# A hybrid decoder layer: two PSUM pools for the whole program, another pairing of the output tiles, and a later second norm

## The chip, the cores and the metric

The kernel runs on one core of one Trainium2 chip. The metric is the device time of one execution in microseconds (us). The kernel before took 1080.27 us, the median of three runs (1080.08, 1080.27, 1080.79). Its profile was taken in one further execution.

## The reference

One layer on x of 1024 tokens x 1024 channels, in fp32:

```python
u = rms_norm(x, norm1_g)
z = u @ w_in                                  # split into a convolution part and a retention part
y = concat(group_norm(conv(z)), group_norm(retention(z)) * silu(gate))
x = x + y @ w_out
h = relu(rms_norm(x, norm2_g) @ w_up)         # w_up is 1024 x 4096
x = x + (h * h) @ w_down                      # w_down is 4096 x 1024
out = rms_norm(x, final_norm_g)
```

The change touches the line with `w_out` (the tiles of x that it finishes), the second norm, and the two products of the MLP.

## The kernel before, in words

**Number format.** All matmuls of the large products take operands that are split into a high and a low part of fp32r. One product of 512 x 512 by 512 x 512 in one call of `mm` (L395 to L403) into one PSUM bank is 12 matmuls of 128 x 512: four slices of the contracted dimension, times high by high, low by high, high by low. The activations' parts are tiles `U` (`V` for the down product, `y` for the out-projection), the weights' parts `wh` and `wl`. A weight piece `r` comes by DMA; ScalarE (ACT) casts it to `wh`, VectorE (DVE) subtracts to get `wl` (`split_piece`, L168). Sums and differences of weight pieces, `r<-r,r`, are GpSimd's (POOL, `Left.split`). Every call to ACT, DVE and POOL goes through a wrapper, so its line in the profile is L74.

**Layout.** x is kept transposed: `x2[i]` holds 128 channels times 1024 tokens, i = 0 to 7, with two token halves `hs[0]` and `hs[1]`.

**The out-projection** is `group(j)` for j = 0 to 3 (L1059), of 8 steps each. Group j finishes the tiles `x2[j]` and `x2[4 + j]`, first over one half of the contraction and then over the other. `out_evac` (L994) adds a bank to x2 on DVE, squares it on ACT, and adds the square to `sums_[half]` on POOL (`t<-t,t`). The dictionary `todo`, by step number 8j + s, then holds the work that prepares the first MLP product. That one is a Strassen-like scheme: x, scaled by the norm's weights but not yet by its factor, is seen as 2 x 2 blocks (token half by tiles 0 to 3 and 4 to 7), and the seven products, in the order 1, 2, 6, 5, 3, 7, 4 (`MLP_ORDER`), take the operands "11", "21", "t2", "t1", "22", "t3", "t4". Each needs four slices, slice j from tiles j and 4 + j. For j = 3 this preparation runs into the MLP's first products: the list `rest` (L1234) gives what is issued behind each of them. The sums `un` go by DVE's `sum1` to `sum4` (L980 on), a high half of U by ACT's `put_hi`, a low half by DVE's `put_lo`.

**The first MLP pass** (L1249 to L1266) computes the up product for two blocks of 256 hidden channels, in 14 products with a bank each, from pools of the two pairs. Here the second norm's factor is found on the way: `token_roots` (L313) sums the 128 partitions of `sums_` by tiny matmuls with a column of ones and takes roots on ACT, `rnorms` takes reciprocals on DVE, `spread` (L339) brings the factors into two PSUM banks, `r_half`, by matmuls with the identity. `Pair.put` multiplies the finished hidden blocks with them; the two banks stay in use until the last block.

**Down products** (L1268, matmuls at L1276) have an inner dimension of 256 each and a Winograd-like scheme, in which x2 itself collects the products in another basis. `new_basis(i)` (L1003) brings tiles i - 1 and i into it: two POOL subtractions of 128 x 512. Tiles that the MLP needs only later are stored to DRAM meanwhile, `put_aside` (a DMA `k<-x`, L1030), to free SBUF, and read again by `fetch_back` (`x<-k`, L1035). Both are on the SP queue, which works in order, as do the weight loads. After this pass, up and down products alternate, and the last block (L1385) multiplies the remaining hidden channels.

**PSUM** has eight banks of 128 x 512 fp32. Until the out-projection's end they are the pools `pm` and `pr` of four each; then both are closed and `pu` (2), `pd` (4) and `pn` (2, for the factors and later the last block) are opened under the names pm, pr and pn. Instructions of each engine run in the order of issue; semaphores between engines are set by the framework from the tiles that are read and written, and a new pool's tiles wait for those of the closed one.

## Time and profile before

| | |
|---|---|
| runs | 1080.27 us median, 1080.08 to 1080.79 |
| profiled execution, device time | 1081.81 us |
| its span, first to last instruction | 1079.0 us |
| matmuls on TensorE (PE) | 4860, mean granted clock 0.997 |
| instructions on DVE, ACT, POOL | 1246, 904, 366 |
| out-projection's last matmul starts | 442.84 us |
| first MLP pass | 443.70 us to about 486.4 us |
| last block's first matmul starts | 1022.00 us |

The busy share of an engine is an average over stages. A line of a timeline has the start in us from the span's start, the length, the engine, line and operation, out<-in by the program's names, the tile's shape and how many instructions are taken together; a bracket gives idle time of that engine just before, and what ended it. Matmuls overlap their neighbours: their starts, not their lengths, give the pace.

### The profile page before, as it was taken

What the parts mean: (1) busy time and instruction counts of PE and PEld (TensorE: products, weight loads), DVE (VectorE), ACT (ScalarE), POOL (GpSimd) and SP (SyncE); (2) the same over time, 40 slices, a digit from 0 to 9 for tenths busy, and PEclk for the clock granted to TensorE, in tenths of its full rate; (3) what the DMA queues carried; (4) which work ended last, traced back from release to release, by engine and by line L of the source; (5) the groups of instructions that cost most, each with busy time, mean ns of one, the idle gap of its engine ahead of it and who ended that gap; (6) DMA issues with size and microseconds to landing.
All of it is one profiled execution on the core that took longest, in us unless ns stands there. A gap on an engine that the chain in (4) does not pass through costs nothing.

```text
span 1079.0 us, 13854 instructions
## 1 busy us (share of the span) xinstructions
PE 1060.5 (98%) x4860; PEld 881.6 (82%) x4860; DVE 878.7 (81%) x1246; ACT 460.2 (43%) x904; POOL 538.0 (50%) x366
## 2 busy tenths in 40 slices
PE   9999999999989999999999999999999999999997
PEld 7888888887768888788788888888888888888886
DVE  7446546799998656699999989989899899899955
ACT  8211445663435544444433443433343344334453
POOL 6234223255753223559538358267276185384552
PEclk9999999999999999999999999999999999999999
DMA  7111122222223635050121211201301301200204
GB/s 274 62 59 39 40 70 78 75 79 73 78 59 118 215 104 188 1 195 21 48 88 39 69 49 49 79 30 57 90 21 50 98 20 50 88 20 20 69 30 156
DMA packets 39685, 82.25 MB, mean 76 GB/s; under 512 B 4544, under 2 KB 5696, under 8 KB 39616
## 3 DMA queue, kind: packets, MB, share of 16 engines
q1 hardware_dynamic: 39328, 80.85, 23.0%
q8 instruction: 38, 0.62, 0.2%
q10 hardware_dynamic: 288, 0.52, 0.1%
q14 instruction: 31, 0.25, 0.1%
HBM read 71.92 MB, written 9.44 MB: 75 GB/s over the span
## 4 chain that ended last, share of the span: by engine, by line
PE 79%; DVE 10%; POOL 4%; issue 3%; ACT 2%; DMA 1%; DVEq 0%; SPq 0%; POOLq 0%; ACTq 0%
PE b L403 46%; PE b L1276 22%; PE b L357 4%; PE b L1385 4%; DVE wl L74 2%; DVE z L74 2%; POOL z L74 1%; POOL r L74 1%; DVE t L74 1%; DVE x L74 1%; DVE U L74 1%; DVE q L74 1%; DVE xs L74 1%; ACT h L74 1%; DVE m L74 1%
## 5 line engine op out<-in xcount | busy, mean ns | idle before, releaser
L403 PE MATMUL b<-U,wh 128*128 128x512 f32 x1024 | 315.8, 390 | 1.8 <-DVE x L74 1.1
L74 ACT CAST wh<-r 128x512 fp32r<-128x512 f32 x286 | 175.9, 620 | 321.2 <-PE b L403 134.5
L74 DVE TENSOR_TENSOR wl<-r,wh 128x512 fp32r<-128x512 f32 x251 | 231.8, 926 | 91.4 <-ACT wh L74 90.5
L74 POOL TENSOR_TENSOR r<-r,r 128x512 f32<-128x512 f32 x136 | 209.9, 1546 | 116.3 <-DVE wl L74 65.6
L1276 PE MATMUL b<-V,wh 128*128 128x512 f32 x784 | 242.0, 389 | 0.5 <-POOL V L74 0.4
L403 PEld LDWEIGHTS b<-U,wh 128*128 128x128 f32 x1024 | 191.8, 188 | 42.6 <-issue 1.9
L74 DVE TENSOR_TENSOR x<-x,b 128x512 f32<-128x512 f32 (+1 forms) x312 | 195.6, 673 | 30.2 <-PE b L1385 14.2
L403 PE MATMUL b<-U,wl 128*128 128x512 f32 x512 | 199.5, 390 | 0.3 <-POOL wl L74 0.3
L1276 PEld LDWEIGHTS b<-V,wh 128*128 128x128 f32 x784 | 147.1, 188 | 32.3 <-POOL V L74 0.8
L74 POOL TENSOR_TENSOR t<-t,t 128x512 f32<-128x512 f32 x70 | 106.4, 1524 | 97.9 <-ACT t L74 51.9
L1276 PE MATMUL b<-V,wl 128*128 128x512 f32 x392 | 152.5, 389 | 0.0
L74 POOL TENSOR_TENSOR wl<-r,wh 128x512 fp32r<-128x512 f32 x35 | 48.6, 1394 | 160.7 <-ACT wh L74 153.5
L403 PEld LDWEIGHTS b<-U,wl 128*128 128x128 f32 x512 | 96.2, 188 | 21.2 <-POOL wl L74 0.7
L403 PE MATMUL b<-uh,wh 128*128 128x512 f32 x304 | 103.4, 399 | 2.3 <-DVE z L74 2.3
L403 PE MATMUL b<-uh,wl 128*128 128x512 f32 x304 | 100.8, 391 | 1.1 <-DVE wl L74 1.1
L403 PE MATMUL b<-ul,wh 128*128 128x512 f32 x304 | 101.0, 392 | 0.0
L1276 PEld LDWEIGHTS b<-V,wl 128*128 128x128 f32 x392 | 73.5, 188 | 15.2
L74 POOL TENSOR_TENSOR V<-t,V 128x512 fp32r<-128x512 f32 x35 | 49.6, 1416 | 67.3 <-ACT V L74 67.3
L74 DVE TENSOR_TENSOR t<-t,b 128x512 f32<-128x512 f32 x112 | 75.8, 677 | 1.7 <-POOL t L74 1.2
L74 ACT ACTIVATE t<-t 128x512 f32<-128x512 f32 x64 | 40.2, 631 | 79.8 <-DVE t L74 79.2
L74 DVE TENSOR_TENSOR V<-t,V 128x512 fp32r<-128x512 f32 x63 | 70.3, 1116 | 0.0
L403 PEld LDWEIGHTS b<-uh,wl 128*128 128x128 f32 x304 | 57.3, 189 | 13.9 <-DVE wl L74 1.5
(178 smaller groups left out, 1422.1 us busy)
## 6 DMA issues: line engine op xcount, KB each, us to landing
r<-w_up_t SPq DMA_DIRECT2D x64, 256.0 KB, 2.6
r<-w_down_t SPq DMA_DIRECT2D x56, 256.0 KB, 2.7
r<-w_in_t SPq DMA_DIRECT2D x48, 256.0 KB, 2.7
xt<-xT SPq DMA_DIRECT2D x16, 256.0 KB, 5.4
xs<-xT SPq DMA_DIRECT2D x8, 512.0 KB, 4.9
r<-w_out_t SPq DMA_DIRECT2D x16, 256.0 KB, 2.7
x<-xT SPq DMA_DIRECT2D x8, 512.0 KB, 8.9
k<-x SPq DMA_DIRECT2D x6, 512.0 KB, 3.2
```

The lines of the kernel that those rows point to most:

```text
L74: return f(out, *args, **kw)
L357: nc.tensor.matmul(vb[i], a[k][:, i * P : (i + 1) * P], b[k // 2][:, vs], start=(k == 0 and a is uh and b is vh), stop=(k == KT - 1 and a ...
L403: nc.tensor.matmul(b, a[:, k, :], rhs(n, k)[r], start=(start and i == 0), stop=(stop and i == len(ops) - 1),)
L1276: nc.tensor.matmul(b, a, r, start=(i == 0), stop=(i == len(ops) - 1))
L1385: nc.tensor.matmul(z, a, b, start=(k == 0 and t == 0), stop=(k == 3 and t == 2))
```

## The change

Three things are changed together; the instructions of each engine are the same in number.

1. `pm` and `pr` of four banks are kept for the whole program. The factors `r_half`, the first two banks of the last block and the two banks `ends` come from `pm`; `r_half` is cleared ahead of the last block.
2. `new_basis(j)` pairs the tiles j and 4 + j, which one group finishes, and not i - 1 and i. It is called in step 8j + 14 for j < 3, followed by the put-asides of both tiles in step 8j + 15; only `new_basis(3)` is left for the MLP pass, behind product 7 (products are counted from 0). Before, `new_basis(1)` stood in step 16, the put-asides of tiles 0 and 1 in step 17, of 2 in step 24 and of 4, 5, 6 in steps 15, 23, 31; and `new_basis` of 7, 5 and 3 stood behind products 7, 8 and 9. `down_take`, the last sums and the host's order of `w_down` follow the new pairs.
3. `token_roots` comes behind product 5 instead of 3, `rnorms` behind 7 instead of 5, `spread` behind 9 instead of 8, and the first two `v_split` one product later.

```diff
-    banks_ = ctx.enter_context(ExitStack())
-    pm = banks_.enter_context(tc.tile_pool(name="pm", bufs=4, space=PSUM))
-    pr = banks_.enter_context(tc.tile_pool(name="pr", bufs=4, space=PSUM))
+    pm = ctx.enter_context(tc.tile_pool(name="pm", bufs=4, space=PSUM))
+    pr = ctx.enter_context(tc.tile_pool(name="pr", bufs=4, space=PSUM))
...
-    def new_basis(i):
+    def new_basis(j):
-        for f, part in ((i - 1, hs[1]), (i, hs[0])):
-            pool.tensor_sub(x2[f][:, part], x2[f][:, part], x2[i][:, hs[1]])
+        for f, part in ((j, hs[1]), (4 + j, hs[0])):
+            pool.tensor_sub(x2[f][:, part], x2[f][:, part], x2[4 + j][:, hs[1]])
...
-            todo[15] = [lambda: put_aside(4 + j)]
+            todo[14] += [lambda: new_basis(j)]
+            todo[15] = [lambda: put_aside(j), lambda: put_aside(4 + j)]
...
-    todo[16] += [lambda: new_basis(1)]
-    todo[17] += [lambda: put_aside(0), lambda: put_aside(1)]
-    todo[24] += [lambda: put_aside(2)]
...
-    banks_.close()
-    pm = ctx.enter_context(tc.tile_pool(name="pu", bufs=2, space=PSUM))
-    pr = ctx.enter_context(tc.tile_pool(name="pd", bufs=4, space=PSUM))
-    pn = ctx.enter_context(tc.tile_pool(name="pn", bufs=2, space=PSUM))
...
-        call(new_basis, 7),
-        call(new_basis, 5),
         call(new_basis, 3),
+        [],
+        [],
+        [],
         [lambda: v_split(early, 1, 0)],
         [lambda: v_split(early, 1, 1)],
-        [],
         [],
...
-        if at == 3:
+        if at == 5:
             roots = [token_roots([sums_[h]], rtok[:, 4 * h : 4 * h + 4]) for h in range(2)]
-        if at == 5:
+        if at == 7:
             wides = [rnorms(r) for r in roots]
-        if at == 8:
-            r_half[:] = [spread(w, pn) for w in wides]
+        if at == 9:
+            r_half[:] = [spread(w, pm) for w in wides]
...
-            quads = [x2[2 * q + f][:, sl] for f in range(2) for sl in hs]
+            quads = [x2[4 * f + q][:, sl] for f in range(2) for sl in hs]
...
+    r_half.clear()
...
-            zs[:4] = [bank(p_) for p_ in (pn, pn, pr, pm)]
+            zs[:4] = [bank(p_) for p_ in (pm, pm, pr, pm)]
...
-    ends = [bank(pn) for _ in range(2)]
+    ends = [bank(pm) for _ in range(2)]
```

Three places show what this does to the engines' instructions (the line numbers of the kernel after are one smaller here; the number after a name is the tile's).

TensorE at the border of the out-projection and MLP product 0, with the semaphores that an instruction waits for, before; `yh` and `yl` are the out-projection's operands, and the `U` rows product 0:

```order
L403 MATMUL b_3804<-yh_3080,wh_3696 128x512
L403 MATMUL b_3804<-yl_3081,wh_3696 128x512
L403 MATMUL b_3804<-yh_3080,wl_3697 128x512
L403 MATMUL b_3887<-U_3249,wh_3795 128x512 [waits DVE_49,PE_49,Activation_49]
L403 MATMUL b_3887<-U_3249,wh_3795 128x512
```

The same rows after:

```order
L402 MATMUL b_3804<-yh_3080,wh_3696 128x512
L402 MATMUL b_3804<-yl_3081,wh_3696 128x512
L402 MATMUL b_3804<-yh_3080,wl_3697 128x512
L402 MATMUL b_3880<-U_3249,wh_3795 128x512 [waits Activation_49]
L402 MATMUL b_3880<-U_3249,wh_3795 128x512
```

Product 0 no longer waits for DVE, only for ACT, which makes its weight piece.

TensorE at the end of product 3, before; `b_3971` is product 3's bank, the `ones` rows are the root sums, `b_4011` is product 4's:

```order
L403 MATMUL b_3971<-U_3802,wh_3863 128x512 x2
L403 MATMUL b_3971<-U_3802,wl_3864 128x512
L313 MATMUL b_3999<-ones,t_3189 128x1 x4
L313 MATMUL b_4005<-ones,t_3190 128x1 x4
L403 MATMUL b_4011<-U_3431,wh_3908 128x512 x2
L403 MATMUL b_4011<-U_3431,wl_3909 128x512
```

After, from the end of product 5; `b_4021` is product 5's bank and `b_4053` product 6's:

```order
L402 MATMUL b_4021<-U_3936,wh_3927 128x512 x2
L402 MATMUL b_4021<-U_3936,wl_3928 128x512
L312 MATMUL b_4041<-ones,t_3189 128x1 x4
L312 MATMUL b_4047<-ones,t_3190 128x1 x4
L402 MATMUL b_4053<-U_3366,wh_3953 128x512 x2
L402 MATMUL b_4053<-U_3366,wl_3954 128x512
```

The root sums stand two products later, between products 5 and 6.

POOL around the end of the out-projection, before; `t` rows add squares to the norm's sums, `r` rows combine weight pieces, `x` rows are `new_basis`:

```order
L74 TENSOR_TENSOR r_3408<-r_3408,r_3406 128x512
L74 TENSOR_TENSOR t_3190<-t_3190,t_3846 128x512
L74 TENSOR_TENSOR r_3594<-r_3594,r_3596 128x512
L74 TENSOR_TENSOR r_3590<-r_3594,r_3590 128x512
L74 TENSOR_TENSOR r_3592<-r_3592,r_3590 128x512
L74 TENSOR_TENSOR t_3190<-t_3190,t_3871 128x512
L74 TENSOR_TENSOR r_3410<-r_3412,r_3406 128x512
L74 TENSOR_TENSOR r_3594<-r_3596,r_3590 128x512
L74 TENSOR_TENSOR x_4037<-x_4037,x_3169 128x512
```

The same place after:

```order
L74 TENSOR_TENSOR r_3408<-r_3408,r_3406 128x512
L74 TENSOR_TENSOR t_3190<-t_3190,t_3846 128x512
L74 TENSOR_TENSOR x_3164<-x_3164,x_3168 128x512
L74 TENSOR_TENSOR x_3168<-x_3168 128x512
L74 TENSOR_TENSOR r_3592<-r_3592,r_3594 128x512
L74 TENSOR_TENSOR r_3588<-r_3592,r_3588 128x512
L74 TENSOR_TENSOR r_3590<-r_3590,r_3588 128x512
L74 TENSOR_TENSOR t_3190<-t_3190,t_3873 128x512
L74 TENSOR_TENSOR r_3410<-r_3412,r_3406 128x512
L74 TENSOR_TENSOR r_3592<-r_3594,r_3588 128x512
L74 TENSOR_TENSOR x_3165<-x_3165,x_3169 128x512
```

The two subtractions of `new_basis(2)` now stand ahead of three weight sums and of the last sum of squares.

## Prediction

> **What bounds the kernel now.** I read the engines' busy time first, then the idle time that TensorE (PE) has inside the reach of the change, then the timeline of each engine around those places. The page's first part:

> ```profile
> PE 1060.5 (98%) x4860; PEld 881.6 (82%) x4860; DVE 878.7 (81%) x1246; ACT 460.2 (43%) x904; POOL 538.0 (50%) x366
> ```

> PE is busy for 1060.5 of 1079.0 us. The change alters no matmul, so it can only win or lose PE's idle time, 18.5 us in all, or PE's clock. The waits from 440 to 530 us (us in total, times, longest), and then those from 1000 to 1030 us:

> ```profile
> PE b L403 <- DVE x L74: 1.1, 2, 0.7
> PE b L403 <- ACT t L74: 0.7, 1, 0.7
> ```
> ```profile
> PE b L1385 <- DVE t L74: 0.4, 1, 0.4
> ```

> These three rows are all that PE waits for in those windows. PE's timeline around the first (start, length, operation, and in brackets the wait before it):

> ```profile
> 442.84 0.39 PE L403 MATMUL b<-yh,wl 128*128 128x512 f32 x1
> 443.70 0.70 PE L403 MATMUL b<-U,wh 128*128 128x512 f32 x2 [0.47 <-DVE x L74]
> 446.31 0.39 PE L403 MATMUL b<-U,wl 128*128 128x512 f32 x1
> 447.36 0.70 PE L403 MATMUL b<-U,wh 128*128 128x512 f32 x2 [0.66 <-DVE x L74]
> ```

> The out-projection ends at 442.84 and the first two MLP products (I call the 14 of the first MLP pass product 0 to 13) each wait until DVE has evacuated the last output tiles, because their pools can only be opened on banks of closed ones. PE's timeline a little later:

> ```profile
> 455.64 1.84 PE L313 MATMUL b<-ones,t 128*128 128x1 f32 x16
> 457.34 0.72 PE L403 MATMUL b<-U,wh 128*128 128x512 f32 x2
> 459.52 0.62 PE L403 MATMUL b<-U,wh 128*128 128x512 f32 x2
> 459.98 0.39 PE L403 MATMUL b<-U,wl 128*128 128x512 f32 x1
> 460.20 0.62 PE L403 MATMUL b<-U,wh 128*128 128x512 f32 x2
> 462.92 0.62 PE L403 MATMUL b<-U,wh 128*128 128x512 f32 x2
> 471.09 1.95 PE L339 MATMUL b<-ident,t 128*128 128x128 f32 x16
> 472.79 0.48 PE L403 MATMUL b<-U,wh 128*128 128x512 f32 x1
> ```

> From 460.20 to 462.92 lies one product: 2.72 us, 0.227 for each of 12 matmuls. The root sums take 455.64 to 457.34, 1.70 us, ahead of product 4; the spread takes 1.70 as well, from 471.09. The pair at 459.52 is the tenth and eleventh matmul of product 4, the first to read the left operand U made from output tile 7, the last tile to be finished. What makes that U, on DVE and then on ACT:

> ```profile
> 449.59 1.78 DVE L74 TENSOR_TENSOR un<-un 128x512 f32<-128x512 f32 x1
> 453.67 0.69 DVE L74 TENSOR_TENSOR wl<-r,wh 128x512 fp32r<-128x512 f32 x1 [2.30 <-ACT wh L74]
> 454.28 0.68 DVE L74 TENSOR_TENSOR U<-un,U 128x512 fp32r<-128x512 f32 x1
> 454.88 1.41 DVE L74 SCALAR_TENSOR_TENSOR un<-x,sm,un 128x512 f32<-128x512 f32 x2
> 457.98 0.69 DVE L74 TENSOR_TENSOR wl<-r,wh 128x512 fp32r<-128x512 f32 x1 [1.69 <-ACT wh L74]
> 458.59 0.68 DVE L74 TENSOR_TENSOR U<-un,U 128x512 fp32r<-128x512 f32 x1
> ```
> ```profile
> 451.40 0.62 ACT L74 CAST U<-un 128x512 fp32r<-128x512 f32 x1 [3.01 <-DVE un L74]
> 456.32 0.62 ACT L74 CAST U<-un 128x512 fp32r<-128x512 f32 x1 [2.69 <-DVE un L74]
> 457.32 0.62 ACT L74 CAST wh<-r 128x512 fp32r<-128x512 f32 x1
> ```

> The high half of this U is ready at 456.94 (456.32 + 0.62) and the low half at 459.27 (458.59 + 0.68). The two engines pass work to and fro, each bracket naming the other, and none names PE. So PE is at its end there by chance: it needs the low half at about 459.75, half a microsecond after it is ready.

> **Part 1, pools for the whole program.** Product 0 takes a bank long free. Then it can follow the last out-projection matmul directly, at 442.84 + 0.23 = 443.07, and product 4, with the roots gone from before it, starts at 443.07 + 4 x 2.72 = 453.95. In before the same four products had ended at 455.64: a gain of 1.69. At the other end of the program pool `pn` goes too. PE's timeline there:

> ```profile
> 1022.00 0.84 PE L1385 MATMUL b<-hid,wd 128*128 128x512 f32 x3
> 1023.20 2.14 PE L1385 MATMUL b<-hid,wd 128*128 128x512 f32 x8 [0.35 <-DVE t L74]
> ```

> The second bank of the last block was held by the factors until the last scaling; the 3 matmuls should take 0.68, so 1022.68 was due and 0.52 is lost, 0.6 with the slower first step after a wait. In after the banks are those of products long taken: -0.6.

> **Part 2, roots two products later.** Their 1.70 are not hidden by anything on PE: they leave the path ahead of product 4 and return ahead of product 6. The roots were cover, though: they gave the U chain time. Product 4 now starts 3.39 earlier (457.34 - 453.95) and comes to its tenth matmul at 453.95 + 2.05 = 456.0. There it waits for the high half until 456.94 at least, and for the low half until 459.27 at least. Product 5 follows the eleventh matmul by 0.45 (two steps), and a semaphore's delay of about 0.1: 459.85 if the chain isn't late, against 460.20. So of the 3.39 only 0.35 is kept, and then the roots are still to come. With d for the lateness of the chain, product 6 starts at 459.85 + d + 2.72 + 1.70 = 464.27 + d, against 462.92: **+1.35 + d**. The later parts (reciprocals after 7 instead of 5, spread after 9 instead of 8) keep their lengths; a product lies between the last of the reciprocals and the spread as before, and the first down product has about 1 us more than its operands need. I cost them at nothing; if that cover went, a wait of up to 1 us would stand ahead of the first down product.

> **Part 3, the pairing.** It makes d. Two POOL subtractions of x now stand before three of r and the last sum t. POOL's timeline:

> ```profile
> 421.79 1.29 POOL L74 TENSOR_TENSOR t<-t,t 128x512 f32<-128x512 f32 x1 [8.06 <-ACT t L74]
> 444.32 1.74 POOL L74 TENSOR_TENSOR t<-t,t 128x512 f32<-128x512 f32 x1
> 446.02 4.79 POOL L74 TENSOR_TENSOR r<-r,r 128x512 f32<-128x512 f32 x3
> 450.78 1.74 POOL L74 TENSOR_TENSOR t<-t,t 128x512 f32<-128x512 f32 x1
> 475.19 1.30 POOL L74 TENSOR_TENSOR x<-x,x 128x512 f32<-128x512 f32 x1 [11.20 <-DMA x<-k]
> ```

> POOL was through at 452.52. With two operations of 1.30 to 1.74 more it is through at 455.1 to 456.0. DVE's two-input operations at 453.67 and 454.28 took 0.69 and 0.68 with POOL idle; the like at 449.59, beside POOL, took 1.78. So d lies between 0 (POOL finishes early) and 1.1 for one operation hit, or 1.4 if the second is caught for a part. I take **1.0**: one hit, by the row at 449.59. [...]

> The same moves touch queues. SP now must wait for POOL before it puts tile 2 aside, until about 448 (446.02 and one operation); behind it stand the put-aside of tile 6, four loads of up weights and two of down weights. Those weights belong to products behind the spread at 471.09, and a put-aside lands soon:

> ```profile
> k<-x SPq DMA_DIRECT2D x6, 512.0 KB, 3.2
> ```

> (The last number is the median us to landing.) So this hides. The put-asides of tiles 1 and 5 wait for POOL's x operations right behind the sum at 421.79, so until 425 or 426; 3.2 more is 429, and ACT first rewrites the buffer here:

> ```profile
> 430.92 0.71 ACT L74 ACTIVATE un<-x,sm 128x512 f32<-128x512 f32 x1
> ```

> That leaves 1.5 us or more; if not, ACT and the chain behind it would be late by the rest. From 475.19 on POOL loses four of its six operations, and the 11.20 us wait for a fetched tile: free time for DVE, which has its backlog later. PE's timeline there:

> ```profile
> 521.62 0.39 PE L403 MATMUL b<-U,wl 128*128 128x512 f32 x1
> 524.66 0.39 PE L1276 MATMUL b<-V,wl 128*128 128x512 f32 x1
> 525.76 0.70 PE L403 MATMUL b<-U,wh 128*128 128x512 f32 x2 [0.71 <-ACT t L74]
> ```

> From 521.62 to 524.66 are 12 steps in 3.04 us instead of 2.72, and the next step takes 1.10 instead of 0.23: 1.2 us lost to banks that are freed late. A PE that comes 2.35 later finds them free: **-1.2** (bound 0.5, if DVE is itself 0.7 late).

> **Part 4, the clock.** PE's wait in product 4 runs from 456.0 to about 460.3 with d = 1.0, with one matmul of 0.4 in it. Three stretches of the trace (us, PE, PEld, DVE, ACT, POOL busy, granted clock):

> ```profile
> 293.60:297.05 3.45, 2.59 (x10) 1.80 (x10) 3.27 (x5) 1.19 (x3) 0.00 (x0) 1.00 0.28 76
> 317.54:320.95 3.41, 1.21 (x6) 0.67 (x4) 3.27 (x4) 0.00 (x0) 0.81 (x1) 1.00 0.54 154
> 320.95:324.36 3.41, 3.30 (x8) 2.62 (x9) 2.51 (x5) 1.75 (x3) 0.56 (x1) 0.50 0.00 0
> ```

> A stretch of 3.41 us with 1.21 of PE work was followed by one at half the clock, in which 8 matmuls took 3.41 us (0.43 each): 3.41 - 8 x 0.227 = 1.6 us lost. After one with 2.59 the clock stayed. The new wait leaves at most 1.4 us of PE work in some 3.41 us however these are laid, nearer to 1.21, so I expect one such stretch. Part of it may fall on the wait or the roots: 0.9 to 1.6, taken **1.3**. [...]

> **The sum.** 1.35 + 1.0 - 1.2 - 0.6 + 1.3 = +1.85 us; in general d + drop - 0.45. The profiled execution took 1081.81 us, its span 1079.0 with 2.8 around it; the median of the runs is 1080.27, 1.5 below. On that: 1080.27 + 1.85 = **1082.1 us**. A measurement of this kernel can tell about 0.2%, 2.16 us, from no change.

> **Rivals.** A is the forecast, from 0.9 to 2.9 by d 0.4 to 1.4 and a drop of 0.9 to 1.6 (and the recovery at 521): chance 0.50, a third of it above 2.16.
> B: no clock drop, as the matmul inside the wait keeps PE awake. Sum 1.35 + 1.0 - 1.8 = +0.5, 1080.8 us. For it: the wait is split in two of about 2 us, and the quoted gap was 2.31 in one. Against it: the window at 317.54 had nearly as much work. Chance 0.25.
> C, on the slower side: POOL delays DVE twice and DVE stays behind, so that the banks at 521 are still late. d = 1.4, drop 1.6, recovery 0.7 instead of 1.2: 1.35 + 1.4 - 0.7 - 0.6 + 1.6 = +3.05, 1083.3 us. With the recovery whole it decides from d + drop = 2.6. For it: POOL may run until 456.0, over both DVE operations; against it: in before only one of such pairs was slowed in full. Chance 0.19.
> D, faster: the U chain comes earlier with PE (its weight pieces wait for banks and PE somewhere earlier), no stall, and DVE, freed of four POOL operations, no backlog. Then 1.69 + 1.2 + 0.6 = 3.5 off: 1076.8 us. Against it: none of the brackets of that chain names PE. Chance 0.06. The change could also fail to remove the wait at 443, if the four `pm` banks were taken; that leaves product 4's wait shorter by as much, and is near B.

> **Numbers.** Slower by over 0.2%: a third of A and C, 0.16 + 0.19 = 0.35. Within: the rest of A, and B, 0.59. Faster: 0.06. The range from 1079.9 (lower half of B) to 1083.5 (above most of C) leaves out rival D, a little of B and the top of C.

> **What would show it.** Right: no wait before product 0 and 1; PE idle twice inside product 4, released by ACT U and DVE U, product 5 at 17.7 us after product 0's start (460.85 - 443.07); the roots after product 5; a stretch of half clock behind; no wait at 521 to 526 plus 2. Wrong, if product 4 runs through, if DVE's operations before it take 0.7 (then d is 0), if the clock stays at 1.00, or if a new wait of over half a microsecond appears after the spread.

## The result, and the profile after

The kernel after took 1082.79 us, the median of nine runs (1082.17 to 1085.51). The kernel before, run beside it, now has 1078.99 us as the median of nine (1077.12 to 1080.79; the three runs that the prediction knew were its slowest). The ratio is 1.0037, with an interval of 1.0026 to 1.0047: slower by 4.0 us, 2.8 to 5.1. The prediction's 1082.1 us is close as a time, but that is luck in part: it started from 1080.27, which is 1.3 us above the median of nine, and added +1.85 us, less than half of the measured difference. It had named the place; the question is where the other half came from.

Two profiled executions can't be laid on each other by their clocks here. After's reached the last matmul of the out-projection at 438.78 us and before's at 442.84, though PE's work up to there is the same. PE's first matmuls of 128x512, in before and then in after, show the larger part (groups of four; the first, second, third and eighth):

```profile
6.56 2.05 PE L357 MATMUL b<-vh,uh 128*128 128x512 f32 x4 [0.87 <-DVE vh L74]
8.40 1.91 PE L357 MATMUL b<-vl,uh 128*128 128x512 f32 x4
10.11 1.20 PE L357 MATMUL b<-vh,ul 128*128 128x512 f32 x4
...
14.80 1.07 PE L357 MATMUL b<-vl,uh 128*128 128x512 f32 x4
```
```profile
5.86 1.48 PE L356 MATMUL b<-vh,uh 128*128 128x512 f32 x4 [0.17 <-DVE vh L74]
7.17 1.08 PE L356 MATMUL b<-vl,uh 128*128 128x512 f32 x4
8.09 1.07 PE L356 MATMUL b<-vh,ul 128*128 128x512 f32 x4
...
12.62 1.07 PE L356 MATMUL b<-vl,uh 128*128 128x512 f32 x4
```

In before the second group still takes 1.71 us (8.40 to 10.11), 0.43 for each matmul; in after it takes 0.92. So the eighth group starts 14.80 - 12.62 = 2.2 us earlier in after's execution. Another 1.5 us is the stretch of half clock that the prediction quoted at 320.95, which after's execution doesn't have, and the remaining 0.4 comes in small steps between them. All this belongs to the execution and not to the kernel: e4 below has the instructions of before up to MLP product 3, and its execution reached the out-projection's last matmul at 440.00. So from here on every time is counted from the start of the last out-projection matmul in the same execution.

What PE waited for in after between 440 and 530 us (us in total, times, longest):

```profile
PE b L402 <- ACT U L74: 4.4, 1, 4.4
PE b L402 <- DVE U L74: 1.8, 1, 1.8
```

The waits for DVE's evacuation and at 525 are gone. Two new ones stand in their place, both in product 4. PE's timeline there:

```profile
438.78 0.39 PE L402 MATMUL b<-yh,wl 128*128 128x512 f32 x1
439.01 0.61 PE L402 MATMUL b<-U,wh 128*128 128x512 f32 x2
...
451.70 0.39 PE L402 MATMUL b<-U,wl 128*128 128x512 f32 x1
456.45 0.50 PE L402 MATMUL b<-U,wh 128*128 128x512 f32 x1 [4.36 <-ACT U L74]
458.78 0.80 PE L402 MATMUL b<-U,wh 128*128 128x512 f32 x1 [1.83 <-DVE U L74]
459.38 0.63 PE L402 MATMUL b<-U,wl 128*128 128x512 f32 x1
459.80 1.05 PE L402 MATMUL b<-U,wh 128*128 128x512 f32 x2
...
464.44 1.84 PE L312 MATMUL b<-ones,t 128*128 128x1 f32 x16
466.14 0.72 PE L402 MATMUL b<-U,wh 128*128 128x512 f32 x2
```

Product 0 follows the out-projection by one step of 0.23. The tenth matmul of product 4, behind the one at 451.70, waits 4.36 us and the eleventh 1.83. From there matmuls come every 0.43 us instead of 0.227. The roots follow product 5, and product 6 starts at 466.14, 27.36 us after the out-projection's last matmul; in before it was 462.92 - 442.84 = 20.08. That is +7.28 us. The prediction had 1.35 + 1.0 + 1.3 = 3.65 for it.

Its chain of DVE and ACT, first DVE then ACT:

```profile
444.96 0.68 DVE L74 TENSOR_TENSOR x<-x,b 128x512 f32<-128x512 f32 x1
447.91 1.77 DVE L74 TENSOR_TENSOR un<-un 128x512 f32<-128x512 f32 x1
451.98 0.78 DVE L74 TENSOR_TENSOR wl<-r,wh 128x512 fp32r<-128x512 f32 x1 [2.30 <-ACT wh L74]
452.68 1.75 DVE L74 TENSOR_TENSOR U<-un,U 128x512 fp32r<-128x512 f32 x1
458.04 0.68 DVE L74 TENSOR_TENSOR U<-un,U 128x512 fp32r<-128x512 f32 x1
```
```profile
427.48 0.61 ACT L74 CAST U<-un 128x512 fp32r<-128x512 f32 x1
431.50 0.73 ACT L74 ACTIVATE U<-x,sm 128x512 fp32r<-128x512 f32 x1 [3.41 <-PE b L402]
432.13 0.61 ACT L74 ACTIVATE t<-x 128x512 f32<-128x512 f32 x1
```

DVE's U<-un takes 1.75 us where it took 0.68: the lateness d of the prediction, in its place and size. But DVE's last evacuation, the row at 444.96, already ends 445.64 - 438.78 = 6.86 us after the out-projection's last matmul; in before the same operation ended at 447.21, 4.37 after it:

```profile
446.54 0.67 DVE L74 TENSOR_TENSOR x<-x,b 128x512 f32<-128x512 f32 x1
```

So 2.5 us of the chain are lost before it comes to the place that the prediction looked at. The ACT rows say where: ACT stands still for 3.41 us, until PE has done some matmuls. It is the ACT operation that writes U "11" of slice 3, which `todo` has in step 8 x 3 + 2 = 26 (the expectations below call it step 28). In before it stood here, with no wait:

```profile
432.04 0.72 ACT L74 ACTIVATE U<-x,sm 128x512 fp32r<-128x512 f32 x1
```

It doesn't read anything that PE makes; it waits for its **output buffer**. A new tile takes an SBUF buffer that an earlier tile gives back. In before the program lays this U where x2 tile 2 was, put aside in step 24. The change puts tile 2 aside in step 31 only, and the program lays this U elsewhere: where the low part of the first `y` slice (`yl`) was, an operand of the out-projection. PE reads that one last in the second matmul of step 29, 34 matmuls of 0.227 us before the out-projection's last at 438.78:

```profile
431.07 0.39 PE L402 MATMUL b<-yl,wh 128*128 128x512 f32 x1
```

It ends at 431.46, and ACT goes on at 431.50.

The clock, in four stretches of after's trace (us, then the busy us of PE, PEld, DVE, ACT and POOL, the granted clock, and the DMA's share and GB/s):

```profile
450.19:453.60 3.41, 1.90 (x9) 1.24 (x7) 1.62 (x2) 1.76 (x4) 3.33 (x3) 1.00 0.80 288
453.60:457.02 3.42, 0.50 (x1) 0.19 (x1) 2.15 (x3) 1.24 (x3) 0.28 (x1) 1.00 0.00 0
457.02:460.43 3.41, 1.65 (x4) 1.36 (x5) 3.00 (x4) 1.42 (x3) 1.65 (x1) 0.50 0.02 5
460.43:463.84 3.41, 3.41 (x9) 2.64 (x9) 3.41 (x4) 1.14 (x2) 2.16 (x2) 0.50 0.27 77
```

One stretch with 0.50 us of PE work, and then two at half clock, not one: the first of these two had only 1.65 us of work itself. From the eleventh matmul to the roots it took 464.44 - 458.78 = 5.66 us; in before, from 459.75 to 462.92, 3.17. So the clock cost 2.5 us.

### The profile page after: what moved, and what is told of

Read it like the earlier page. It is cut to its first block, busy times and chain, and to the rows that moved or that the text cites. A ratio compares the mean times of both kernels' runs of the same rounds, so it can differ in the third digit from the quotient of the medians.

```text
span 1080.5 us, 13854 instructions
## 1 busy us (share of the span) xinstructions
PE 1058.8 (98%) x4860; PEld 881.3 (82%) x4860; DVE 883.3 (82%) x1246; ACT 460.3 (43%) x904; POOL 539.7 (50%) x366
## 4 chain that ended last, share of the span: by engine, by line
PE 82%; DVE 8%; issue 3%; POOL 3%; ACT 2%; DMA 1%; SPq 0%; DVEq 0%; POOLq 0%; ACTq 0%
PE b L402 46%; PE b L1269 24%; PE b L356 4%; PE b L1379 4%; DVE z L74 2%; POOL z L74 1%; DVE U L74 1%; POOL r L74 1%; DVE xs L74 1%; DVE wl L74 1%; DVE q L74 1%; ACT h L74 1%; DVE m L74 1%; POOL wl L74 1%; PE b L338 0%
## 5 line engine op out<-in xcount | busy, mean ns | idle before, releaser
L74 ACT CAST wh<-r 128x512 fp32r<-128x512 f32 x286 | 176.2, 620 | 334.3 <-PE b L402 144.7
L74 DVE TENSOR_TENSOR wl<-r,wh 128x512 fp32r<-128x512 f32 x251 | 234.2, 935 | 90.3 <-ACT wh L74 89.4
L74 POOL TENSOR_TENSOR r<-r,r 128x512 f32<-128x512 f32 x136 | 210.1, 1547 | 133.0 <-DVE wl L74 80.4
L74 DVE TENSOR_TENSOR x<-x,b 128x512 f32<-128x512 f32 (+1 forms) x312 | 195.5, 673 | 26.9 <-PE b L1379 15.7
L74 POOL TENSOR_TENSOR t<-t,t 128x512 f32<-128x512 f32 x70 | 106.9, 1531 | 97.2 <-ACT t L74 50.8
L74 POOL TENSOR_TENSOR wl<-r,wh 128x512 fp32r<-128x512 f32 x35 | 49.1, 1408 | 159.4 <-ACT wh L74 152.1
L74 POOL TENSOR_TENSOR V<-t,V 128x512 fp32r<-128x512 f32 x35 | 48.6, 1389 | 67.8 <-ACT V L74 67.8
L74 DVE TENSOR_TENSOR t<-t,b 128x512 f32<-128x512 f32 x112 | 75.8, 677 | 1.7 <-POOL t L74 1.2
L74 ACT ACTIVATE t<-t 128x512 f32<-128x512 f32 x64 | 40.1, 630 | 70.3 <-DVE t L74 69.6
L74 DVE TENSOR_TENSOR V<-t,V 128x512 fp32r<-128x512 f32 x63 | 68.1, 1081 | 0.0
## 6 DMA issues: line engine op xcount, KB each, us to landing
xs<-xT SPq DMA_DIRECT2D x8, 512.0 KB, 5.1
x<-xT SPq DMA_DIRECT2D x8, 512.0 KB, 7.6
k<-x SPq DMA_DIRECT2D x6, 512.0 KB, 3.0
```

The source lines that it names most:

```text
L74: return f(out, *args, **kw)
```

## The experiments

My theory after reading the trace: 2.5 us of the loss are the buffer, 1.0 is POOL before DVE (d), 2.5 is the clock, and the roots give the chain's time away. The rival: the roots' new place alone makes the wait, whatever the buffer. The first four kernels undo one thing or do one part alone.

**e1, the early put-aside of tile 2 in the kernel after.** `new_basis` takes a second argument here, which of its two subtractions to do:

```diff
+    todo[24] += [lambda: new_basis(2, (0,)), lambda: put_aside(2)]
...
-            todo[14] += [lambda: new_basis(j)]
-            todo[15] = [lambda: put_aside(j), lambda: put_aside(4 + j)]
+            todo[14] += [lambda: new_basis(j, (1,) if j == 2 else (0, 1))]
+            todo[15] = [lambda: put_aside(4 + j)] if j == 2 else [lambda: put_aside(j), lambda: put_aside(4 + j)]
```

> The kernel after, with one thing undone: the first subtraction of new_basis(2) and the put-aside of tile 2 come in step 24 again (the second subtraction stays in step 30). Theory (buffer): after's ACT waits 3.4 us in step 28, because the tile U that it writes there got the SBUF buffer of an out-projection operand, and tile 2's buffer, which it had before, is now given back only in step 31; that makes the whole U chain 2.5 us late, and the late POOL subtractions another 1.0. Then here ACT's wait is under 0.7 us, PE's two waits in product 4 shrink from 4.4 + 1.8 to about 2 + 2 us, at most one stretch of half clock follows, and the time is 2.5 to 4 us below the kernel after, so 0 to +1.9 us against before. Rival (roots): the wait is there because the roots no longer cover the chain, whatever the buffer; the time stays within 0.7 us of after, +3.1 to +4.5 us against before.

Measured: ratio to before 1.0005 (0.9995 to 1.0015), so 3.4 us below after by the ratios. The same ACT operation, and PE's waits in product 4:

```profile
429.77 0.72 ACT L74 ACTIVATE U<-x,sm 128x512 fp32r<-128x512 f32 x1 [0.71 <-DMA k<-x]
```
```profile
453.73 0.49 PE L402 MATMUL b<-U,wh 128*128 128x512 f32 x1 [0.87 <-ACT U L74]
456.06 0.80 PE L402 MATMUL b<-U,wh 128*128 128x512 f32 x1 [1.84 <-DVE U L74]
```

ACT now waits 0.71 for the put-aside's DMA, a hair over the 0.7 that was expected, and not 3.41 for PE. One stretch of half clock follows. The first wait of PE is 0.87 us and not 2: one of POOL's two subtractions has left the place as well, and DVE's U<-un took 0.69. So e1 undoes the buffer and d together. e7 parts them.

**e2, part 1 alone; e3, part 2 alone; e4, part 3 alone**, each in the kernel before, with the diffs of the section on the change.

> The kernel before with part 1 alone: two pools of four banks for the whole program, the roots, the spread and the pairing as before. Theory (buffer): no wait before products 0 and 1, a wait of 1 to 2 us in product 4 for the low half of U, which takes back all but 0.35 of the 1.69 us; the wait of 0.5 us in the last block gone; the loss of 1.2 us at 521 as before or larger by the 0.35. Sum -0.4 to -1.0 us against before. Rival (pools): a bank that the factors hold in pm costs more than it gives: +1 us or more, with new waits of PE for DVE in the MLP.

Measured: 0.9993 (0.9985 to 1.0002), -0.8 us, with an interval that includes no change at all. The rival's +1 us is out. The wait in product 4 is 1.12 us. The waits that before had from 521 to 526 are still there, now from 519 to 523, and a new one of 0.68 stands at 505:

```profile
505.23 0.70 PE L402 MATMUL b<-U,wh 128*128 128x512 f32 x2 [0.68 <-DVE t L74]
519.30 0.70 PE L1271 MATMUL b<-V,wh 128*128 128x512 f32 x2 [0.22 <-DVE x L74]
523.01 0.70 PE L402 MATMUL b<-U,wh 128*128 128x512 f32 x2 [0.72 <-ACT t L74]
```

> The kernel before with part 2 alone: the new pairing, its put-asides in steps 15, 23 and 31, and only new_basis(3) in the MLP pass; pools and roots as before. Theory (buffer): ACT waits about 3.4 us for PE in step 28, the last evacuations are 2.5 us late, so PE waits about 3 us before product 0 or 1 in all instead of 1.1, and for the late U in product 4 another 0.5 us. With the 1.2 us at 521 regained: +1.5 to +2.5 us against before. Rival (roots): the pairing alone costs little, 0 to +0.5 us, since the roots before product 4 cover the chain.

Measured: 1.0024 (1.0014 to 1.0034), +2.6 us. ACT's and PE's waits, with the roots where they had been:

```profile
432.98 0.73 ACT L74 ACTIVATE U<-x,sm 128x512 fp32r<-128x512 f32 x1 [3.41 <-PE b L403]
```
```profile
443.59 0.70 PE L403 MATMUL b<-U,wh 128*128 128x512 f32 x2 [2.94 <-DVE x L74]
447.26 0.70 PE L403 MATMUL b<-U,wh 128*128 128x512 f32 x2 [0.66 <-DVE x L74]
```

The same 3.41 us of ACT. The lateness of 2.5 appears here as a longer wait before product 0, 2.94 instead of 0.47. The rival's 0 to +0.5 is out. The +2.6 is a little above the theory's 2.5; a wait of 0.56 us for a weight piece ahead of product 8 (at 469.80) wasn't in its sum.

> The kernel before with part 3 alone: root sums behind product 5, reciprocals behind 7, spread behind 9, and the first two V splits one product later; pools and pairing as before. Theory (buffer): product 4 starts 1.70 us earlier and waits about 1.3 us for the low half of U; product 6 starts 1.35 us later than in before, and of this 1.2 comes back at 521: 0 to +0.5 us against before, clock at 1.00 around it. Rival (roots): the missing cover is what costs, +2 us or more with a stretch of half clock.

Measured: 1.0010 (1.0001 to 1.0018), +1.1 us: above the theory's 0.5, far from the rival's 2. Product 4 waits 1.26 us for U and product 6 starts 1.42 later than in before, as expected; two things weren't in the sum. A wait of 0.53 us for POOL's V stands inside the first down product, before its fifth matmul at 489.52, and only 0.74 of the 1.23 us at 521 came back.

**e5, parts 1 and 2 with the early put-aside, the roots as before.**

> Parts 1 and 2 with the early put-aside of tile 2 (as in e1), and the root sums, reciprocals and spread behind products 3, 5 and 8 as before. Theory (buffer and backlog): the roots lie in the time that product 4 would wait for its U anyway, so product 4 waits about 1.1 us for the low half as in e2, the clock stays at 1.00 there, and with POOL freed of four subtractions at 475 to 484 DVE is less behind at 500 to 526, where e2 lost 2.1 us: 0 to 1.2 lost here. Sum -1.5 to -3 us against before, below both kernels. Rival: what makes the loss at 500 to 526 is only that PE comes early, not POOL; then it is 2.1 us again and the time is that of e2, -0.4 to -0.9 us against before.

Measured: 1074.93 us (median of seven), ratio 0.9970 (0.9959 to 0.9981): 3.2 us below before, the only kernel that is clearly faster. The clock stays at 1.00 there, as expected. Its one wait of PE between 440 and 530 us:

```profile
PE b L402 <- DVE U L74: 1.1, 1, 1.1
```

**e6, the kernel after with PE kept busy.** The filler multiplies a U tile that lies ready into a spare bank; i counts product 4's matmuls from 0.

```diff
+            for m in range({9: 18, 10: 8}.get(i, 0)):
+                nc.tensor.matmul(spare, u[:, :P], u, start=True, stop=True)
```

> The kernel after with 26 additional matmuls, whose result nobody reads, in PE's two waits in product 4: 18 (4.1 us) ahead of the tenth matmul, 8 (1.8 us) ahead of the eleventh. Everything else as in after, the late ACT and POOL steps too. Theory (clock): after loses 2.4 us to two stretches of 3.41 us at half clock, which follow because PE does next to nothing in 6.6 us; with the filler the clock stays at 1.00 and the time is 1.5 to 2.5 us below after, +1.5 to +2.5 against before. Rival (chain alone): PE at half clock is hidden behind the late U chain and DVE's work; the clock stays up, but the time is within 0.5 us of after, +3.3 to +4.3 against before.

Measured: 1.0014 (1.0005 to 1.0023), +1.5 us against before, 2.5 below after. The chain is as late as in after, but PE's clock stays up:

```profile
453.40:456.80 3.40, 3.26 (x15) 2.37 (x13) 2.90 (x3) 0.47 (x1) 1.02 (x1) 1.00 0.06 19
456.80:460.20 3.40, 3.19 (x13) 2.34 (x14) 2.21 (x3) 2.20 (x5) 1.44 (x1) 1.00 0.00 0
```

**e7, e1 with one more POOL operation.**

```diff
+    todo[30] += [lambda: pool.tensor_sub(un[2][:, hi_], x2[6][:, hs[0]], x2[6][:, hs[1]])]
```

> e1 (the kernel after with the early put-aside of tile 2) with one more POOL subtraction of 128x512, into a half tile that nobody reads any more, behind the second one in step 30: two POOL operations stand there, as in after, while the buffer is the early one. Theory (POOL is the d of the prediction): DVE's two-input operations before product 4's U meet POOL again, U's low half is 0.5 to 1.4 us later than in e1 from the out-projection's end, and the time is 0.5 to 3 us above e1, by whether another stretch of half clock follows. Rival: all of after's lateness came from the buffer; U's low half is within 0.2 us of e1's, and so is the time.

Measured: 1.0020 (1.0008 to 1.0031), 1.6 us above e1 by the ratios. The intervals of the two overlap a little, so the trace has to carry it. DVE, and PE in product 4:

```profile
449.92 1.77 DVE L74 TENSOR_TENSOR U<-un,U 128x512 fp32r<-128x512 f32 x1
```
```profile
453.73 0.50 PE L402 MATMUL b<-U,wh 128*128 128x512 f32 x1 [2.13 <-ACT U L74]
456.06 0.50 PE L402 MATMUL b<-U,wh 128*128 128x512 f32 x1 [1.83 <-DVE U L74]
```

The table counts all from the start of the out-projection's last matmul (438.29 in e7, 439.55 in e1). "Tenth" is product 4's tenth matmul; "end" is the start of the program's last matmul.

| kernel | PE's waits in product 4 | stretches at half clock there | tenth | product 6 | end | ratio of times to before |
|---|---|---|---|---|---|---|
| before | none | 0 | 16.68 | 20.08 | 628.67 | 1 |
| after | 4.36 + 1.83 | 2 | 17.67 | 27.36 | 634.07 | 1.0037 |
| e1, early put-aside | 0.87 + 1.84 | 1 | 14.18 | 22.86 | 629.58 | 1.0005 |
| e2, pools | 1.12 | 0 | | 19.80 | 628.77 | 0.9993 |
| e3, pairing | 0.47 | 0 | | 23.33 | 631.42 | 1.0024 |
| e4, roots | 1.26 | 0 | | 21.50 | 630.27 | 1.0010 |
| e5, pools and pairing | 1.08 | 0 | | 19.80 | 626.37 | 0.9970 |
| e6, filler | 0.34 | 0 | 17.73 | 25.08 | 631.78 | 1.0014 |
| e7, POOL operation | 2.13 + 1.83 | 1 | 15.44 | 24.37 | 631.36 | 1.0020 |

From e1 to e7 the tenth matmul comes 1.26 us later: POOL. From e7 to after another 2.23: the buffer. From after to e6 product 6 comes 2.28 earlier: the clock, which against before's pace cost 2.5 (e6 is itself 0.2 behind that pace). With the 1.35 that the roots' move was forecast to cost, 1.35 + 1.26 + 2.23 + 2.5 = 7.3, and after's product 6 was 7.28 later than before's.

One more pair is worth reading: e1 and e5 differ by part 3 alone. With the buffer's loss undone in both, the later roots make the end 629.58 - 626.37 = 3.2 us later and the ratio 0.0035 larger. So with the early put-aside it is the move of the roots, with the stretch at half clock that its wait brings, that takes back the gain of the other two parts.

The ends differ from before by 0.2 to 1.6 us more than the ratios of times say; before has one profiled execution, and what of this is that execution's own stays open.

## Why the prediction was right or wrong, by its steps

- **Part 1, pools: right.** Product 0 starts 0.23 us behind the out-projection, product 4 at 449.89 (eight steps before 451.70), 11.11 us after it, as forecast (453.95 - 442.84). The wait in the last block is gone. Alone the pools bring less than a microsecond, if anything (e2), because the chain of U holds product 4, and banks that are freed late hold PE at 505 to 523.
- **Part 2, roots: right in mechanism.** They were the cover of the chain, and moving them makes product 4 wait: e4 has product 6 at +1.42, and +1.35 was forecast. "I cost them at nothing" failed for the cover behind the spread: e4 shows a wait of 0.53 us in the first down product, within the one microsecond that the prediction priced it at. After, e1 and e5, with the new pairing, show no such wait.
- **Part 3, d: right.** 1.0 was taken; DVE's operation took 1.75 us in after where it had taken 0.68, and e7 against e1 shows 1.26 at the tenth matmul. In after POOL's operation ran from 452.16 to 453.88 and DVE's beside it from 452.68 to 454.43, so DVE ended 0.55 us behind POOL.
- **Part 3, "So this hides": wrong, and the step that failed.** The prediction asked of the put-asides when their data would be rewritten, for tiles 1 and 5, and when the loads behind them are needed. It didn't ask who takes the buffer that tile 2 gives back. That taker is ACT's U "11" of slice 3; it gets another buffer, ACT waits 3.41 us for PE, and everything behind it is 2.2 to 2.5 us late. In the sum this was a term put at nothing. e3 shows the wait without the other parts, and e1 and e7 show the loss go with the order of put-asides.
- **Part 4, clock: right that it falls, too small.** 1.3 was taken for one stretch, at most 1.6. The longer wait made it two, 2.5 us (e1 and e7, with shorter waits, have one); e6 takes them away and gains 2.5 us in the times. Rival B, that the one matmul inside the wait keeps the clock up, falls.
- **The 1.2 us at 521: right as a number, wrong as a cause.** The number was worked out from PE coming late; POOL's relief was named, but not taken as the cause. In e4 PE is late by 1.4 us and 0.49 us is still lost; in e5 PE comes 0.3 us earlier than in before, and nothing is lost. e2, which differs from e5 by the pairing and its put-asides alone, has the waits. So it is the pairing that removes them. That it does so because POOL, with four subtractions fewer there, disturbs DVE less is the likely reason, and wasn't tried by itself. The traces point that way; the same DVE operation beside POOL's subtractions in e2, and with POOL idle in e5:

```profile
475.96 1.78 DVE L74 TENSOR_TENSOR V<-t,V 128x512 fp32r<-128x512 f32 x1
```
```profile
474.87 0.68 DVE L74 TENSOR_TENSOR V<-t,V 128x512 fp32r<-128x512 f32 x1
```

- **Sum:** 1.35 + 1.0 - 1.2 - 0.6 + 1.3 was forecast; with the buffer's 2.2, d of 1.26 and the clock's 2.5 it is 1.35 + 2.2 + 1.26 - 1.2 - 0.6 + 2.5 = 5.5, and the trace shows 634.07 - 628.67 = 5.4. The runs say 4.0, with 5.1 at most, so the trace's terms are somewhat too large or before's profiled execution was somewhat short behind the out-projection. That 1082.1 us came so near is luck: the forecast left out the buffer's 2.2 us, took half of the clock's loss, and started 1.3 us too high. Rival C's +3.05 is nearer to the measured difference, but not for its reason, a DVE that stays behind at 521; what was missing was the buffer, which no rival named.

## What to carry to other kernels

When a change moves the place where a tile is given back, list the next tiles that are allocated and say which buffer each gets then and who last uses it: a wait for a buffer shows up at an instruction whose inputs the change never touched. Before removing work from an engine's path, ask for whom that work was the cover; here most of the roots' time stood where PE would have waited anyway (e5 keeps them there and is the fastest). And an idle stretch on PE can have a second price, the slow matmuls that follow: here 2.5 us behind waits of 6.2.

## What the runs showed of the hardware

```profile
313.66:317.07 3.41, 2.52 (x12) 1.75 (x10) 3.34 (x4) 0.00 (x0) 2.12 (x2) 1.00 0.47 144
317.07:320.49 3.42, 2.00 (x9) 1.66 (x10) 2.64 (x4) 0.57 (x1) 0.00 (x0) 1.00 0.19 72
```

Stretches with 0.50 (after) and, in e7 and e1, with 1.04 and 1.18 us of work were followed by half clock:

```profile
453.20:456.60 3.40, 1.04 (x3) 0.67 (x4) 1.89 (x3) 2.51 (x5) 1.12 (x1) 1.00 0.00 0
```
```profile
452.17:455.58 3.41, 1.18 (x5) 0.41 (x3) 1.72 (x4) 2.52 (x5) 0.09 (x1) 1.00 0.00 0
```

Of these stretches and before's, the one with 1.21 us (before) is the fullest that was followed by half clock; with 1.70 (after, 1071.42 to 1074.83) and 1.90 (after, 450.19 to 453.60) the next one had the full clock. What comes between 1.21 and 1.70 isn't shown. Of the stretches at half clock, the one with 1.65 us of work (after, 457.02 to 460.43) was followed by another at half clock; those with 2.93 (e1, 455.58 to 458.99), 3.30 (before, 320.95 to 324.36) and 3.41 (after, 460.43 to 463.84) were followed by the full clock. The drop at 318, worth 1.5 us, is in before's profiled execution and not in after's. What made the start's 2.2 us isn't shown: the clock column gives 1.00 there in both, and the slow pace is read from the matmuls' starts alone. Together the two are some 4 us between these two profiles, which is the size of the spread among before's own runs (1077.12 to 1080.79).
